# Eighteen products of an output projection moved between the last attention head's steps, and the second norm's product moved to GpSimd and ScalarE

## The chip, the cores and the metric

The kernel runs on one core of a Trainium2 chip. The metric is the device time of one execution in microseconds; the lower the better. A profile names the engines PE (TensorE, its weight loads apart as PEld), DVE (VectorE), ACT (ScalarE), POOL (GpSimd) and SP (SyncE, which here only issues DMAs).

## The reference

A decoder block on 1024 tokens of width 1024, one layer, all in float32:

```python
xn = rmsnorm(h, norm_mix_g);  proj = xn @ w_in
att = forgetting_attention(q, k, v, log_f)        # 8 heads of 64, causal, softmax
sg  = chunked_spatial_gating(u, vg, ...)          # gMLP, chunks of 128
h = h + concat([att, sg]) @ w_out                 # the output projection
h = h + conv_ffn(rmsnorm(h, norm_ffn_g), ...)     # D_FF = 2816
return rmsnorm(h, norm_final_g)
```

The change lies at the end of the attention, in the output projection and in the norm in front of the ConvFFN.

## The kernel before, in words

**Precision.** Every large product is done in three passes: each operand is split into a rounded high part and a low part, and high x high, high x low and low x high are summed in PSUM. So one product of a 128x128 block with 512 columns is three matmul instructions.

**The heads.** Eight heads run one behind the other, five steps each (`STEPS`, 40 in all, `n` from 0 to 39, head `h = n // 5`). A step turns up to two groups of softmax rows for the next step (`turn_p`: four transposes into a PSUM bank, L1026, a high part by ScalarE, L1027, a low part by VectorE, L1028, both into a `pt` buffer, of which there are three), and multiplies the groups of this step by V (`values`, L1042). While a head is worked on, the logits of the next one are made in the steps' gaps (`logits_mm`, L978 and L979; `logits_min` on VectorE, L991; `logits_exp` on ScalarE, L1001). The last head's steps, 35 to 39, have no next head: nothing stands between their turns and products. All PE instructions here are chained by hand in program order (`seq`). PSUM has eight banks: two `place()` tiles of two banks each for logits (tag `L`), and four `bank()` tiles (tag `b`).

**The row tail.** Behind step 37's products, the last head's reciprocal row sums are transposed (L940), copied (L941), stored to HBM (L942) and loaded back as a broadcast (L943). `pair_half(3, ...)` then multiplies the pair of heads 6 and 7 by them and splits the result: L956 on VectorE, L957 on ScalarE, L958 on VectorE, second token half first. The result, `attT[3]`, is the fourth of the four operands of the attention's part of the output projection.

**The output projection.** `wmm(tt, hf, ps, ks_)` (L1279 to L1281) multiplies the token tile `tt` (eight of 128 tokens) with the column half `hf` (512 columns) of the weights `wo[k]`; `k` = 0 to 3 are the four pairs of heads, three products each. The gating's part was done earlier and lies in HBM as `hpd`. `wo_load` (L1087) loads weights and has POOL split them (L1098, L1099). All eight banks are taken (`psb` is released, `psc` opened) and the tiles 0, 4, 1, 5 (`first`) run their k = 0, 1, 2 ahead into them: 72 products. Then, in the order 0, 4, 1, 5, 2, 3, 6, 7, each tile gets its last products, VectorE adds `hpd` per half (`hadd`, L1289), and `norm2` makes the second norm: ScalarE squares with a row sum (L1296) and takes the root (L1297), VectorE inverts it (L1298) and multiplies the tile by it and by the gain in one operation (L1299). `flip` of the tile before turns the normed tile with eight transposes (L1317) and spreads it by ScalarE and VectorE (L1303 to L1334) into operands of a Strassen-like product of the ConvFFN.

**Ahead for the ConvFFN.** `upw_a` and `upw_b` load the first two blocks of up weights; `split` makes high and low parts of A11 and A12 (ScalarE L160, VectorE L166, four of each, called before and after the 72 products); with `inplace`, POOL makes their eight sums (L1251 to L1253 and L1259). The ConvFFN's first products are L1372.

**Order.** Each engine works its queue in order. What the program writes is a list; a scheduler of the framework orders each engine's queue by program order and by its own estimate of what is ready. `after(tc, later, earlier)` forces an order within it. A tile of a pool can be used again when everything that reads or writes it is done.

Of the kernel before, what the change touches and what calls it, by code (L numbers as in the profile page):

```python
# [69 lines left out]
def block_kernel(ctx: ExitStack, tc: tile.TileContext, xT, xtok, wuv, wv0, wva, wvk, wvl, wqk, cpk, bfv,  # L70
# [1030 lines left out]

    STEPS = [[(h, g) for g in GROUPS[n:n + 2]] for h in range(8) for n in range(0, 9, 2)]
# [35 lines left out]
    for n, step in enumerate(STEPS):  # L1138
# [63 lines left out]
    psa.release()  # L1202
    psa = tc.alloc_tile_pool(name="psc", bufs=4, space=bass.MemoryType.PSUM, reuse_waits="tile")
# [39 lines left out]
    def upw_b(i, out, inplace=False):  # L1243
# [5 lines left out]
        if inplace:  # L1249
            s = [a21, ut_(upl, "sg", [P, 512], F32, 4), a11, a12]  # L1250
            pool.tensor_tensor(out=a11, in0=a21, in1=a11, op=ALU.add)  # L1251
            pool.tensor_tensor(out=s[1], in0=a11, in1=a22, op=ALU.add)
            pool.tensor_tensor(out=a21, in0=a21, in1=a22, op=ALU.add)  # L1253
# [5 lines left out]
        pool.tensor_tensor(out=s[3], in0=s[1], in1=a12, op=ALU.add)  # L1259
# [13 lines left out]
    normed = {}  # L1273

    def wmm(tt, hf, ps, ks_):
        ts_ = slice(tt * P, (tt + 1) * P)
        for k in ks_:
            w = wo[k][hf]
            pe.matmul(ps, attT[k][:, 0, ts_], w[:, 0, :], start=(k == 0), stop=False)  # L1279
            pe.matmul(ps, attT[k][:, 0, ts_], w[:, 1, :], start=False, stop=False)  # L1280
            pe.matmul(ps, attT[k][:, 1, ts_], w[:, 0, :], start=False, stop=(k == 3))  # L1281
# [5 lines left out]
    def hadd(tt, hf, ps):  # L1287
        o = slice(hf * 512, hf * 512 + 512)
        x = dve.tensor_tensor(out=h2[tt][:, o], in0=ps, in1=h2[tt][:, o], op=ALU.add)  # L1289
        if tt == 5:  # L1290
            after(tc, x, normed[1])

    def norm2(tt):
        xn[tt] = ut_(xtp, "xn", [P, 1024], F32, 2)
        r = ss2[:, tt:tt + 1]
        act.activation(xn[tt], h2[tt], AF.Square, accum_out=r)  # L1296
        act.activation(r, r, AF.Sqrt, bias=eps[:, 0:1], scale=1.0 / 1024)  # L1297
        dve.reciprocal(r, r)  # L1298
        normed[tt] = dve.scalar_tensor_tensor(out=xn[tt], in0=h2[tt], scalar=r, in1=g2b, op0=ALU.mult, op1=ALU.mult)  # L1299
# [9 lines left out]
    def flip(tt):  # L1309
# [3 lines left out]
        for kh in range(2):  # L1313
            ps = sbank()
            for j in range(4):
                k = 4 * kh + j
                pe.transpose(ps[:, j * P:(j + 1) * P], xn[tt][:, k * P:(k + 1) * P], ident)  # L1317
# [18 lines left out]

    WA = [upw_a(i) for i in range(AHEAD)]
# [481 lines left out]
```

## Time and profile before

| | |
|---|---|
| median of 3 runs | 1049.43 us (1049.25 to 1049.82) |
| the profiled execution | 1049.38 us |
| its span, first to last instruction | 1047.7 us |
| granted TensorE clock, mean | 0.999 |

How to read the profile: its page gives the busy time of every engine as a share of the span; the view by windows gives it for a stretch of time, in us from the span's start; the timeline gives single instructions (start, duration, engine, line, operation, output <- inputs, shape, count when several are merged, and in brackets the idle time before and what ended it). `SPq` and `ACTq` are the queues that issue DMAs. A matmul's shown duration overlaps the next one's, so its price is the distance between starts.

### The profile page before, as it was taken

The page shows a single profiled execution, that of the slowest core. Times are in us where ns is not written, and L with a number is a line of the kernel's source. Part 1 is how long each engine was busy: PE and PEld are TensorE (multiplying, and loading weights), DVE is VectorE, ACT ScalarE, POOL GpSimd, SP SyncE. Part 2 cuts the span into 40 slices and gives each one's busy share as a digit, 9 for nine tenths or more (in the row PEclk, how much of TensorE's full clock was granted, in tenths as well). Part 3 has the DMA queues.
Part 4 walks back from the last instruction along what each step waited for, and adds up shares of the span by engine and source line. Part 5 has one row for each costly group of instructions (what it writes and reads, how often), then busy time and mean ns, then how long its engine had stood idle before and what let it go on. Part 6 is the DMA issues. An engine that isn't in the chain of part 4 may idle for free.

```text
span 1047.7 us, 14269 instructions
## 1 busy us (share of the span) xinstructions
PE 1037.6 (99%) x4998; PEld 869.5 (83%) x4998; DVE 891.8 (85%) x1302; ACT 563.4 (54%) x1003; POOL 217.7 (21%) x165
## 2 busy tenths in 40 slices
PE   9999999999999999999999999999999999999997
PEld 6988888988888888788888888888888888888886
DVE  6898887888888779998999989898997866897774
ACT  6777632457767747644444444444444544454654
POOL 0000241500422540253333323323331000000000
PEclk9999999999999999999999999999999999999999
DMA  9622558795745533232254431432322998333432
GB/s 326 237 87 86 159 155 245 224 260 174 205 138 171 184 139 141 80 103 79 96 174 162 131 121 60 131 121 70 131 81 81 320 336 297 105 98 101 142 119 101
DMA packets 67451, 161.66 MB, mean 154 GB/s; under 512 B 8094, under 2 KB 9238, under 8 KB 67380
## 3 DMA queue, kind: packets, MB, share of 16 engines
q1 hardware_dynamic: 67108, 160.72, 47.7%
q8 instruction: 39, 0.64, 0.3%
q14 instruction: 32, 0.26, 0.1%
q10 hardware_dynamic: 272, 0.04, 0.0%
HBM read 115.68 MB, written 45.05 MB: 153 GB/s over the span
## 4 chain that ended last, share of the span: by engine, by line
PE 92%; DVE 3%; DMA 2%; ACT 1%; issue 1%; SPq 1%; ACTq 0%; DVEq 0%
PE k L1632 20%; PE qc L1372 11%; PE qa L1372 11%; PE qd L1372 11%; PE qb L1372 5%; PE ps L270 5%; PE pb L270 5%; PE pb L1042 3%; PE pb L1026 2%; PE qc L510 2%; PE qa L510 2%; PE qd L510 2%; PE pl L979 2%; PE pl L978 2%; PE pf L1066 1%; PE pf L1068 1%
## 5 line engine op out<-in xcount | busy, mean ns | idle before, releaser
L1632 PE MATMUL k<-whb,wha 128*128 128x512 f32 (+1 forms) x936 | 209.9, 386 | 0.0
L1632 PEld LDWEIGHTS k<-whb,wha 128*128 128x128 f32 x936 | 174.1, 188 | 35.8 <-DVE wha L166 0.2
L1372 PE MATMUL qc<-xT,whb 128*128 128x512 f32 x540 | 129.9, 389 | 0.1
L1372 PE MATMUL qa<-xB,wha 128*128 128x512 f32 x528 | 127.4, 390 | 0.0
L1372 PEld LDWEIGHTS qc<-xT,whb 128*128 128x128 f32 x540 | 101.3, 188 | 21.6 <-ACT whb L160 0.5
L1372 PEld LDWEIGHTS qa<-xB,wha 128*128 128x128 f32 x528 | 98.8, 188 | 20.8 <-DVE wha L166 0.4
L160 ACT CAST wha<-sg 128x512 fp32r<-128x512 f32 x77 | 47.8, 622 | 96.9 <-PE k L1632 83.9
L160 ACT CAST whb<-sg 128x512 fp32r<-128x512 f32 x82 | 50.6, 618 | 87.3 <-PE qc L1372 67.1
L166 DVE TENSOR_TENSOR wha<-sg,wha 128x512 fp32r<-128x512 f32 x77 | 52.8, 687 | 39.2 <-ACT wha L160 39.1
L1372 PE MATMUL qd<-xB,whb 128*128 128x512 f32 x264 | 63.7, 389 | 0.0
L1372 PE MATMUL qd<-xT,whb 128*128 128x512 f32 x264 | 63.7, 389 | 0.0
L1372 PE MATMUL qb<-xT,whb 128*128 128x512 f32 x252 | 61.0, 389 | 0.0
L166 DVE TENSOR_TENSOR whb<-sg,whb 128x512 fp32r<-128x512 f32 x82 | 57.0, 697 | 4.4 <-ACT whb L160 4.3
L1027 ACT CAST pt<-pb 128x512 fp32r<-128x512 f32 x72 | 40.4, 584 | 37.5 <-PE pb L1026 32.5
L1256 POOL TENSOR_TENSOR sg<-raw 128x512 f32<-128x512 f32 x20 | 30.8, 1541 | 140.3 <-DVE whb L166 78.1
L1372 PEld LDWEIGHTS qd<-xT,whb 128*128 128x128 f32 x264 | 49.5, 188 | 10.5 <-DVE u L1479 0.3
L1372 PEld LDWEIGHTS qd<-xB,whb 128*128 128x128 f32 x264 | 49.6, 188 | 10.3
L1028 DVE TENSOR_TENSOR pt<-pb,pt 128x512 fp32r<-128x512 f32 x72 | 47.4, 687 | 10.7 <-ACT pt L1027 10.4
L1372 PEld LDWEIGHTS qb<-xT,whb 128*128 128x128 f32 x252 | 47.2, 188 | 10.0 <-DVE whb L166 0.3
L1042 PE MATMUL pb<-pt,V 128*128 128x512 f32 (+3 forms) x192 | 49.6, 362 | 0.4 <-DVE pt L1028 0.3
L1259 POOL TENSOR_TENSOR sg<-sg,raw 128x512 f32<-128x512 f32 x20 | 33.3, 1667 | 63.5 <-DVE whb L166 63.5
L1257 POOL TENSOR_TENSOR sg<-sg,raw 128x512 f32<-128x512 f32 x20 | 34.8, 1740 | 47.5 <-issue 44.9
(426 smaller groups left out, 2241.1 us busy)
## 6 DMA issues: line engine op xcount, KB each, us to landing
raw<-wup SPq DMA_DIRECT2D x44, 512.0 KB
sg<-hx SPq DMA_DIRECT2D x77, 256.0 KB
hx<-hs SPq DMA_DIRECT2D x44, 256.0 KB
hx<-ca SPq DMA_DIRECT2D x35, 256.0 KB
xT<-wdn SPq DMA_DIRECT2D x28, 256.0 KB
x<-kd SPq DMA_DIRECT2D x24, 256.0 KB
A<-xtok SPq DMA_DIRECT2D x8, 512.0 KB
raw<-wqk SPq DMA_DIRECT2D x8, 512.0 KB
```

The lines of the kernel that those rows point to most:

```text
L160: act.copy(h, src)
L166: return eng.tensor_tensor(out=l, in0=src, in1=f32(h), op=ALU.subtract)
L270: pe.matmul(banks[m], xs(n, xi, k)[:, ms], w[:, wi, :], start=(first and k == 0 and c == 0 and (own or m % 2 == 0)), stop=(k == 3 and c == ...
L510: pe.matmul(ps, w[:, wi, ks], xs(n, xi, k), start=(first and c == 0), stop=(c == 11), skip_group_check=True)
L1027: casts.append(act.copy(pt[:, 0, :], ptr))
L1028: los.append(dve.tensor_tensor(out=pt[:, 1, :], in0=ptr, in1=f32(pt[:, 0, :]), op=ALU.subtract))
L1042: seq(pe.matmul(po[half][:, o:o + w], lhs, pt[:, s, c:c + w], start=(new and s == 0), stop=(s == 1 and (half, k) in ((1, 6), (0, 3))), ski ...
L1256: pool.tensor_tensor(out=s[0], in0=a21, in1=a22, op=ALU.add)
L1257: pool.tensor_tensor(out=s[1], in0=s[0], in1=a11, op=ALU.add)
L1259: pool.tensor_tensor(out=s[3], in0=s[1], in1=a12, op=ALU.add)
L1372: pe.matmul(ps, w[:, wi, ks], xb[:, xi, k, :], start=(first and n == 0), stop=(n == 11), skip_group_check=True)
L1632: pe.matmul((banks[bk + m] if ps is None else ps)[:, o], xh[:, xi, ms], wh[:, wi, o], start=((first and p_ == 0 or new) and n == 0), stop= ...
```

## The change

1. **Early products.** `wmm` moves ahead of the steps and takes an `order` function. A table `EARLY` puts products of token tile 0 behind three steps, chained like the rest: behind step 34, k = 0 and 1 of both halves (12 products), behind step 36, k = 2 of half 0 (3), behind step 37, k = 2 of half 1 (3). They accumulate in `place()` tiles: the logits' last ones are read in step 33 and 34.
2. **Weights.** `wo_load((0, 1))` is called at step 33 and `wo_load((2, 3))` at step 34 behind `pair_half(2, ...)`; both were called at step 35.
3. **PSUM.** `psb` stays until the end of the projection. Each token tile has one 1024-column place (`half_of`), of which there are two; `first` has two tiles (0 and 4) in place of four, so 36 products can run without `attT[3]`. The square writes its (unused) output into the tile's place instead of `xn`. `flip` takes `bank()` tiles and is ordered behind given products; tile 0's flip stands behind the first half of tile 1.
4. **The norm's product.** `hadd` has POOL multiply each half by the gain (`gained`) behind VectorE's sum; `norm2` has ScalarE scale the whole by the inverse root (`Copy` with `scale`). VectorE's L1299 goes.
5. **The weight sums on POOL.** The eight in-place sums are held in `parts` and issued two at a time behind the gain products of tiles 1, 5, 2 and 3.

```diff
+    EARLY = {34: ((0, 0, (0, 1)), (0, 1, (0, 1))), 36: ((0, 0, (2,)),), 37: ((0, 1, (2,)),)}
+    def half_of(tt, hf):
+        if tt not in wide:
+            wide[tt] = place()
+        return wide[tt][:, hf * 512:hf * 512 + 512]
...
-        if h == 7 and s == 0:
+        if n == 33:
             for _ in filler:
                 pass
             wo_load((0, 1))
-            wo_load((2, 3))
...
+        if n == 34:
+            wo_load((2, 3))
...
         fill((h, s))
+        for tt, hf, ks_ in EARLY.get(n, ()):
+            wmm(tt, hf, half_of(tt, hf), ks_, lambda m: seq(m) or m)
+            done.update((tt, hf, k) for k in ks_)
...
-    psa.release()
-    psa = tc.alloc_tile_pool(name="psc", bufs=4, space=bass.MemoryType.PSUM, reuse_waits="tile")
...
-            pool.tensor_tensor(out=a11, in0=a21, in1=a11, op=ALU.add)
-            pool.tensor_tensor(out=s[1], in0=a11, in1=a22, op=ALU.add)
-            pool.tensor_tensor(out=a21, in0=a21, in1=a22, op=ALU.add)
+            sums_ = ((a11, a21, a11), (s[1], a11, a22), (a21, a21, a22), (a12, s[1], a12))
+            ops = [lambda o=o: pool.tensor_tensor(out=o[0], in0=o[1], in1=o[2], op=ALU.add) for o in sums_]
+            parts.extend((ops[:2], ops[2:]))
...
     def hadd(tt, hf, ps):
         o = slice(hf * 512, hf * 512 + 512)
-        x = dve.tensor_tensor(out=h2[tt][:, o], in0=ps, in1=h2[tt][:, o], op=ALU.add)
-        if tt == 5:
-            after(tc, x, normed[1])
+        dve.tensor_tensor(out=h2[tt][:, o], in0=ps, in1=h2[tt][:, o], op=ALU.add)
+        if hf == 0:
+            xn[tt] = ut_(xtp, "xn", [P, 1024], F32, 2)
+        gained[tt] = pool.tensor_tensor(out=xn[tt][:, o], in0=h2[tt][:, o], in1=g2b[:, o], op=ALU.mult)
...
-        act.activation(xn[tt], h2[tt], AF.Square, accum_out=r)
+        act.activation(wide[tt], h2[tt], AF.Square, accum_out=r)
         act.activation(r, r, AF.Sqrt, bias=eps[:, 0:1], scale=1.0 / 1024)
         dve.reciprocal(r, r)
-        normed[tt] = dve.scalar_tensor_tensor(out=xn[tt], in0=h2[tt], scalar=r, in1=g2b, op0=ALU.mult, op1=ALU.mult)
+        act.activation(xn[tt], xn[tt], AF.Copy, scale=r)
...
-    first = (0, 4, 1, 5)
-    banks8 = {(tt, hf): (bank() if hf == 0 else sbank()) for tt in first for hf in range(2)}
+    first = (0, 4)
     for hf in range(2):
         for tt in first:
-            wmm(tt, hf, banks8[tt, hf], (0, 1, 2))
+            wmm(tt, hf, half_of(tt, hf), [k for k in range(3) if (tt, hf, k) not in done])
...
         for hf in range(2):
-            if tt in first:
-                wmm(tt, hf, banks8[tt, hf], (3,))
-                hadd(tt, hf, banks8[tt, hf])
-            else:
-                ps = bank()
-                wmm(tt, hf, ps, range(4))
-                hadd(tt, hf, ps)
+            m = wmm(tt, hf, half_of(tt, hf), (3,) if tt in first else range(4))
+            hadd(tt, hf, half_of(tt, hf))
+            if tt == 1 and hf == 0:
+                flip(0, m)
         norm2(tt)
-        if prev is not None:
-            flip(prev)
+        if prev:
+            flip(prev, m)
         prev = tt
+        if tt in (1, 5, 2, 3):
+            for o in parts.pop(0):
+                after(tc, o(), gained[tt])
...
+    psa.release()
+    psa = tc.alloc_tile_pool(name="psc", bufs=4, space=bass.MemoryType.PSUM, reuse_waits="tile")
```

More of the change, by code (lines that the diff above doesn't have):

```diff
@@ L1100, in wo_load, with wmm @@
             wo.append(w)
+    def wmm(tt, hf, ps, ks_, order=lambda m: m):
+        ts_, m = slice(tt * P, (tt + 1) * P), None
+        for k in ks_:
+            w = wo[k][hf]
+            order(pe.matmul(ps, attT[k][:, 0, ts_], w[:, 0, :], start=(k == 0), stop=False))
+            order(pe.matmul(ps, attT[k][:, 0, ts_], w[:, 1, :], start=False, stop=False))
+            m = order(pe.matmul(ps, attT[k][:, 1, ts_], w[:, 0, :], start=False, stop=(k == 3)))
+        return m
+    def half_of(tt, hf):
[3 more added lines that the diff above has]
+    EARLY = {34: ((0, 0, (0, 1)), (0, 1, (0, 1))), 36: ((0, 0, (2,)),), 37: ((0, 1, (2,)),)}
+    wide, done, gained = {}, set(), {}
     STEPS = [[(h, g) for g in GROUPS[n:n + 2]] for h in range(8) for n in range(0, 9, 2)]
@@ L1258, in upw_b @@
             pool.tensor_tensor(out=s[2], in0=a21, in1=a11, op=ALU.add)
-        pool.tensor_tensor(out=s[3], in0=s[1], in1=a12, op=ALU.add)
+            pool.tensor_tensor(out=s[3], in0=s[1], in1=a12, op=ALU.add)
         src = {"A22": a22, "S1": s[0], "S2": s[1], "S3": s[2], "S4": s[3]}
@@ L1272, in block_kernel @@
     xn = [None] * 8
[L1273 to L1281, printed above, removed]
     def hload(tt):
@@ L1307, in hl_of, with flip @@
         lo_of(n, c, src)
-    def flip(tt):
+    def flip(tt, floor=None):
         c = slice((tt % 4) * P, (tt % 4) * P + P)
@@ L1313, in flip @@
         for kh in range(2):
-            ps = sbank()
+            ps = bank() if floor is not None else sbank()
             for j in range(4):
                 k = 4 * kh + j
-                pe.transpose(ps[:, j * P:(j + 1) * P], xn[tt][:, k * P:(k + 1) * P], ident)
+                t = pe.transpose(ps[:, j * P:(j + 1) * P], xn[tt][:, k * P:(k + 1) * P], ident)
+                if floor is not None:
+                    after(tc, t, floor)
             pp.append(ps.rearrange("p (k t) -> p k t", k=4))
```

2 lines of the change are left out of this document (1 added, 1 removed).

## Prediction

> **What bounds the kernel now.** I read the page first, then the busy time by stage, then TensorE's timeline around the last head, then what it waited for there.
>
> ```profile
> span 1047.7 us, 14269 instructions
> PE 1037.6 (99%) x4998; PEld 869.5 (83%) x4998; DVE 891.8 (85%) x1302; ACT 563.4 (54%) x1003; POOL 217.7 (21%) x165
> ```
> ```profile
> 351.00:361.00 10.00, 8.77 (x56) 6.96 (x55) 7.67 (x14) 7.36 (x17) 4.57 (x5) 1.00 0.48 149
> 361.00:371.00 10.00, 10.00 (x45) 8.25 (x45) 6.66 (x10) 5.38 (x9) 2.61 (x2) 1.00 0.63 231
> 383.00:410.00 27.00, 26.99 (x143) 22.25 (x142) 25.42 (x42) 18.01 (x37) 0.00 (x0) 1.00 0.56 195
> 410.00:431.00 21.00, 21.00 (x102) 17.37 (x102) 20.00 (x28) 15.14 (x24) 0.00 (x0) 1.00 0.07 26
> 431.00:451.00 20.00, 19.87 (x86) 15.70 (x85) 19.19 (x24) 12.30 (x17) 9.10 (x5) 1.00 0.40 130
> ```
> The columns after the window are its length, then busy time (and instructions) of PE, PEld, DVE, ACT, POOL, then the granted clock (1.00 everywhere here). PE is the bound, and the only stretch with a visible hole is 351 to 361, the last head's steps. Behind it the output projection (from 360.8) runs without a hole. The profiled execution took 1049.38 us, the median is 1049.43, so the sum is made on 1049.38.
>
> Two rows of the chain of work give PE's pace: a 512-column product costs 5.47/24 = 0.228 us, a transpose 0.87/8 = 0.109.
>
> ```profile
> 416.87 0.87 PE ps L1317 x8
> 417.74 5.47 PE qa L1372 x24
> ```
> ```profile
> 350.36 0.77 PE L1042 MATMUL pb<-pt,V 128*128 128x384 f32 x4
> 350.96 0.62 PE L1026 MATMUL pb<-ident,H 128*128 128x128 f32 x4
> 352.48 0.66 PE L1026 MATMUL pb<-ident,H 128*128 128x128 f32 x4 [0.89 <-DVE pt L1028]
> ...
> 358.05 0.27 PE L940 MATMUL pb<-ident,rs 128*8 128x128 f32 x1
> ...
> 360.37 0.61 PE L1042 MATMUL pb<-pt,V 128*128 128x384 f32 x3 [0.28 <-DVE pt L1028]
> 360.82 0.45 PE L1279 MATMUL pb<-whl,A 128*128 128x512 f32 x1
> ```
> ```profile
> PEld pb L1026 <- DVE pt L1028: 1.4, 2, 1.1
> ...
> PEld pb L1042 <- DVE pt L1028: 0.7, 2, 0.5
> PEld pb L1042 <- ACT pt L1027: 0.4, 1, 0.4
> ```
> From 350.96 to 360.82 PE does 29 transposes (steps 36 to 39 and the row tail's) and value products worth 18 of 512 columns: 29 x 0.109 + 18 x 0.228 = 7.3 us in 9.9. The wait rows (in total, times, longest) show where. So **about 2.5 us is all that can be filled**: some 1.3 around 352 (four transposes are through at 351.40, the next start at 352.48), 0.3 ahead of 356.6, and 0.7 to 0.9 in step 39.
>
> **The change, part by part.**
>
> *Eighteen products move into the head.* They are 18 x 0.228 = 4.1 us of PE, taken out of the stage from 360.82. Their place must be free and their operands there:
>
> ```profile
> 350.41 0.53 DVE L991 CUSTOM_DVE_ANT_0 gg<-pl,t,lim 128x256 f32<-128x256 f32 x1
> ```
> ```profile
> 344.77 0.33 SPq L1090 DMA_DIRECT2D raw<-woa  x1
> 345.80 2.56 POOL L1099 TENSOR_TENSOR whl<-raw,whl 128x512 fp32r<-128x512 f32 x2
> 349.42 2.54 POOL L1099 TENSOR_TENSOR G<-raw,G 128x512 fp32r<-128x512 f32 x2
> 353.00 2.57 POOL L1099 TENSOR_TENSOR G<-raw,G 128x512 fp32r<-128x512 f32 x2
> ```
> The logits place of j=1 is read until 350.94, as step 34's last value product goes out; weights 0 and 1 are split by 348.4, weight 2 by 352.0, and loading them a step or two sooner in the program keeps that. SP issues the last of these loads at 344.77, and an earlier issue only lets its queue go on sooner; the work on POOL is the same.
>
> Twelve products behind step 34 take 2.74 us and push everything behind them. The chain they meet is PE's own order:
>
> ```profile
> 353.84 0.59 ACT L1027 CAST pt<-pb 128x512 fp32r<-128x512 f32 x1 [0.43 <-PE pb L1042]
> ```
> That cast waits for a `pt` buffer (three of them), that is for a value product two groups back, so ScalarE and VectorE cannot run ahead while PE does the twelve. The pause of 1.3 around 352 is covered, the rest (1.4) is delay. The three products of step 36 add 0.68 and the pause of 0.3 goes: at the row tail, behind 15 early products (3.4 us), PE is 3.4 - 1.5 = **1.9 late**. The three of step 37 add 0.68; step 39 still waits for the cast and low part of transposes that are late too, and I give back 0.1. The head ends 2.5 late, at 363.3: of 4.1 us, 1.6 are hidden.
>
> *The wait for the last head's rows.* From the row tail to the projection's fourth product:
>
> ```profile
> 358.64 0.27 ACTq L942 DMA_DIRECT2D rsd<-t  x1
> 360.82 0.45 SPq L943 DMA_DIRECT2D H<-rsd  x1
> 364.96 1.29 DVE L956 TENSOR_TENSOR H<-H 128x512 f32<-128x512 f32 x2 [2.64 <-DMA H<-rsd]
> 365.69 1.22 ACT L957 CAST G<-H 128x512 fp32r<-128x512 f32 x2 [2.56 <-DVE H L956]
> 366.34 1.29 DVE L958 TENSOR_TENSOR G<-H,G 128x512 fp32r<-128x512 f32 x2
> 366.81 2.18 ACT L160 CAST wha<-raw 128x512 fp32r<-128x512 f32 x4
> 367.55 4.68 DVE L166 TENSOR_TENSOR wha<-raw,wha 128x512 fp32r<-128x512 f32 x4
> ```
> Tile 0 uses the second half of these: high part at 366.91, low part at 367.63. Before, 72 products (16.4 us) lie ahead of the first one that needs them, so nobody waits. After, only two 1024-column places exist, so 36 products can run without the fourth weight, and 18 of those are spent: PE arrives at 363.3 + 4.1 = 367.4. The rows come 1.9 late: 368.8 and 369.55. PE waits 1.4, does two products, waits 0.25 more: **+1.65**. Bounds: 0.7 if tile 4 (first half) goes first; 2.5 if the row transfer, now issued closer to the load of the first `h2` tile, lands up to 0.8 later.
>
> *The wait for a place.* Tile 1 cannot start before tile 0's place is given back, and that is now after two sums and the square, which writes into the place. In the trace this chain is:
>
> ```profile
> 378.11 0.69 DVE L1289 TENSOR_TENSOR pt<-pb,pt 128x512 f32<-128x512 f32 x1 [5.87 <-PE pb L1281]
> 378.79 0.69 DVE L1289 TENSOR_TENSOR pt<-ps,pt 128x512 f32<-128x512 f32 x1
> ```
> ```profile
> 379.51 1.06 ACT L1296 ACTIVATE xn<-pt 128x1024 f32<-128x1024 f32 x1 [10.52 <-DVE pt L1289]
> ```
> First sum to end of square: 2.46 us. Tile 0's last product is out at 370.5, tile 4's six follow until 371.85. But on VectorE the four low parts of the up weights (L166) stand right behind L958 in the order of before; there they had 6 us of room, now the sums queue behind them: 369.55 + 4 x 0.6 = 372.0, and tile 1 starts at 372.0 + 2.46 = 374.5. **+2.6**. If the sums go ahead of them, only hadd 0.69 and square 1.06 stand behind 370.5, and 0.5 is left. I take 2.6: the order of before is the nearest row. From tile 1 on each place has 24 products (5.5 us) to be emptied in, so no more of this.
>
> *The norm's product.* Off VectorE go eight of 1.28; onto POOL come sixteen of 1.29 (the L1251 family's unhindered duration), onto ScalarE eight of about 1.06:
>
> ```profile
> L1299 DVE SCALAR_TENSOR_TENSOR xn<-pt,ss,g2b 128x1024 f32<-128x1024 f32 x8 | 10.2, 1280 | 0.1
> L1296 ACT ACTIVATE xn<-pt 128x1024 f32<-128x1024 f32 x8 | 8.5, 1064 | 14.1 <-DVE pt L1289 14.1
> ```
> The longer route (sum 0.69, product 1.29, scaling 1.06, some 1.5 of queue) is hidden by a tile's 5.5 us of products, except perhaps at tile 0, whose flip comes 2.74 us after tile 1 starts. VectorE was 25.42 of 27 us busy from 383 to 410 and never held PE for long, so PE gains nothing there directly. It can gain what little PE loses up to 451: 86 products and 19.87 us in the last window, some 0.4. Moving POOL's eight sums costs nothing if they are done by 415. I take -0.4 for all this; bounds -1.0 (every such gap goes) and +1.0 (the collisions below).
>
> **Sum:** -4.1 + 2.5 + 1.65 + 2.6 - 0.4 = +2.25: 1049.38 + 2.25 = **1051.6 us**.
>
> A collision speaks against the move. While POOL added two SBUF tiles, VectorE's L166 with two SBUF inputs went slow, four in 4.68 us where the neighbour L958 takes 1.29 for two, and POOL's own took 1.67 for 1.29; the sum L1289 of 378.79, with one input from PSUM, kept 0.69 beside POOL:
>
> ```profile
> 368.32 1.67 POOL L1251 TENSOR_TENSOR raw<-raw,raw 128x512 f32<-128x512 f32 x1 [12.75 <-DVE wha L166]
> ...
> 378.45 1.29 POOL L1259 TENSOR_TENSOR raw<-sg,raw 128x512 f32<-128x512 f32 x1
> ```
> Each such meeting cost VectorE (4.68 - 2.6)/2 = 1.0 us. In tiles 4 to 7 four VectorE operations each have two SBUF inputs; if all 16 met POOL, that is 16 us, more than the 10.2 taken off. [...]
>
> **Rivals.**
> *Sums first* (0.20): the scheduler puts tile 0's sums ahead of the up weights' low parts, or tile 4 first. Then 0.5 stands for 2.6: +0.15, **1049.5**. For it: tile 0's first sum has its product some 2 us before the splits end. Against: the splits come sooner in the program.
> *The pauses are filled and no new wait arises* (0.13): the one that ends not slower. Its place is the arrival of the last head's rows: if the two transfers and the two waits behind them fit into the 18 products left, -4.1 + 2.5 - 0.4 = -2.0, **1047.4**. It decides from the point where the rows are there by 367.4, that is 1.4 us sooner than I work out. Against: 358.05 to 366.91 is 8.9 us, PE's work between is 7.4.
> *VectorE and POOL block each other* (0.14): a flip waits for a late product and PE with it, at +1.4 beyond my -0.4 end: 2.25 + 1.4 = +3.65, **1053.0**. For it: the rows above. Against: PE has 5.5 us per tile to spare.
> *The change does not do what it says* (0.03): the early products wait for weights and the head is only longer, some +4: 1053.4. Against: the weights' rows.
>
> **How the numbers follow.** The forecast has 0.50. About 0.2% (2.1 us, 1051.5) is what a measurement of this kernel can tell from no change, and the forecast lies next to that edge: of its 0.50 I put 0.34 slower and 0.16 same. Sums first: all same. Pauses filled: 0.06 faster, 0.07 same. The last two: 0.17 slower. Faster 0.06, same 0.43, slower 0.51. The range leaves out most of the full gain and the worst blocking: 1048.4 to 1053.6. The forecast's own range is 1050.6 to 1052.6.
>
> **What would show it.** In the profile after: eighteen L1279 to L1281 products before the last value product, the hole at 352 gone, the first product behind the head near 363.3 (right if 363.0 to 363.7); PE idle 1 to 2 us just before the fourth weight's first product, released by ScalarE's L957; PE idle again 1.5 to 3 us before tile 1, released by the square; VectorE's sums of tile 0 behind all four L166. I am wrong if tile 1 starts before 373, or if PE has holes at the flips, or if the rows are there before PE.

## The result, and the profile after

| | before | after |
|---|---|---|
| median | 1049.44 us (1049.25 to 1049.82, 4 runs) | 1062.05 us (1059.79 to 1063.38, 4 runs) |
| the profiled execution | 1049.38 us | 1059.79 us |
| its span | 1047.7 us | 1058.1 us |
| granted TensorE clock, mean | 0.999 | 0.997; in the three other runs 0.995 |

After/before is 1.0118 (95%: 1.0105 to 1.013): the kernel became slower by some 12.6 us, where +2.25 was forecast. The page of after opens with

```profile
span 1058.1 us, 14299 instructions
PE 1040.5 (98%) x4998; PEld 870.9 (82%) x4998; DVE 886.1 (84%) x1294; ACT 571.5 (54%) x1011; POOL 237.1 (22%) x181
```

PE has the same 4998 matmuls, so what was added must be idle time or slower products. Both can be read off. First the view of waits for PE from 360 to 480 (total us, times, longest). Before, it has one row:

```profile
PE pb L1042 <- DVE pt L1028: 0.3, 1, 0.3
```

After, in the same window:

```profile
PE pl L1106 <- DVE pt L1299: 3.9, 3, 2.0
PE qc L1386 <- DVE u L1497: 2.0, 1, 2.0
PE pl L1106 <- ACT pl L1306: 1.6, 3, 0.8
PE pl L1106 <- ACT G L957: 1.4, 1, 1.4
PE qa L1386 <- ACT pl L1306: 1.1, 1, 1.1
```

They add up to 10.0 us. Then the clock: of the stretches behind the head, by windows (columns as in the prediction), one stands out:

```profile
351.00:361.00 10.00, 10.00 (x64) 8.78 (x63) 5.93 (x10) 5.71 (x14) 3.55 (x4) 1.00 0.42 132
361.00:371.00 10.00, 7.95 (x34) 5.28 (x32) 6.48 (x11) 6.11 (x11) 0.00 (x0) 1.00 0.68 238
374.60:378.20 3.60, 3.50 (x9) 2.71 (x10) 0.35 (x3) 2.89 (x7) 3.40 (x3) 0.54 0.78 271
383.00:410.00 27.00, 26.25 (x130) 21.04 (x129) 18.85 (x28) 17.12 (x31) 21.05 (x16) 1.00 0.40 137
410.00:431.00 21.00, 18.61 (x93) 15.13 (x92) 13.14 (x22) 16.05 (x28) 4.65 (x4) 1.00 0.13 51
```

The hole of 351 to 361 is gone (8.77 busy before, 10.00 now). The next ten microseconds, full before, now have 2 us of holes. And from 374.7 on PE ran slow products: they start 0.427 us apart in place of 0.228, and nine of them take 3.75 us (374.70 to 378.45) in place of 2.05, which is 1.7 us more.

The view counts idle time only. By starts (the distance from the start before, less 0.228) the same waits are 11.5 us. In the head, 2.1 us of pauses were filled: it took 2.50 us longer, but holds 20 products more, the eighteen and two of the next ones that slipped in (361.49 and 361.72 below), and 20 x 0.228 - 2.50 = 2.06. So 11.5 of waits + 1.7 of slow products - 2.1 = 11.1. From step 34's last value products to the end of the span the kernel takes 11.3 us more (349.42 to 1058.1, before 350.36 to 1047.7), so nearly all is found. The two spans differ by only 10.4, because after came to the head 0.94 us sooner: it lacks 1.0 us of waits in its first ten microseconds (L270), where the profiles of both kernels and of the experiments differ by as much. Times in two profiles can be compared only after such a shift.

The rest of the median's distance, 1062.05 - 1059.79 = 2.3 us, goes with the lower clock of the other three runs: 0.002 of 1058 us is 2.1 us, about one more such stretch. Those runs have no trace, and their mean clock also counts the end of the kernel, where PE has no work left and the granted clock is 0.50, so that is inferred.

PE's timeline around the places shows who ended each wait (in brackets):

```profile
361.49 0.40 PE L1106 MATMUL pl<-whl,A 128*128 128x512 f32 x1
361.72 0.39 PE L1107 MATMUL pl<-whl,A 128*128 128x512 f32 x1
361.95 0.59 PE L1042 MATMUL pb<-pt,V 128*128 128x384 f32 x3
362.38 0.45 PE L1108 MATMUL pl<-whl,A 128*128 128x512 f32 x1
...
367.65 0.47 PE L1106 MATMUL pl<-G,G 128*128 128x512 f32 x1 [1.40 <-ACT G L957]
368.74 0.65 PE L1108 MATMUL pl<-G,G 128*128 128x512 f32 x2
369.92 0.50 PE L1106 MATMUL pl<-G,G 128*128 128x512 f32 x1 [0.53 <-DVE pt L1299]
370.49 0.39 PE L1108 MATMUL pl<-G,G 128*128 128x512 f32 x1
372.92 0.50 PE L1106 MATMUL pl<-G,G 128*128 128x512 f32 x1 [2.04 <-DVE pt L1299]
374.70 0.65 PE L1106 MATMUL pl<-whl,A 128*128 128x512 f32 x1 [0.82 <-ACT pl L1306]
375.15 0.63 PE L1107 MATMUL pl<-whl,A 128*128 128x512 f32 x1
375.58 0.63 PE L1108 MATMUL pl<-whl,A 128*128 128x512 f32 x1
```

And VectorE and ScalarE there:

```profile
369.17 0.69 DVE L1299 TENSOR_TENSOR pt<-pl,pt 128x512 f32<-128x512 f32 x1 [0.33 <-PE pl L1108]
369.78 2.49 DVE L166 TENSOR_TENSOR wha<-raw,wha 128x512 fp32r<-128x512 f32 x4
372.18 1.28 DVE L1299 TENSOR_TENSOR pt<-pl,pt 128x512 f32<-128x512 f32 x2
373.50 1.03 ACT L1306 ACTIVATE pl<-pt 128x1024 f32<-128x1024 f32 x1 [3.31 <-DVE pt L1299]
```

Tile 4's first half comes first. The product at 369.92 writes the second half of a place; it started only when the sum of the first half (369.17) had read it. The product at 372.92 does the same in the other place, whose first sum stands behind the four low parts (L166). Then tile 1 waits for the square at 373.50. That one is tile 4's: it starts ahead of the last of the four sums (373.93), and tile 0's square follows at 374.65.

### The profile page after: what moved, and what is told of

Read it like the earlier page. It is cut to its first block, busy times and chain, and to the rows that moved or that the text cites. A ratio compares the mean times of both kernels' runs of the same rounds, so it can differ in the third digit from the quotient of the medians.

```text
span 1058.1 us, 14299 instructions
## 1 busy us (share of the span) xinstructions
PE 1040.5 (98%) x4998; PEld 870.9 (82%) x4998; DVE 886.1 (84%) x1294; ACT 571.5 (54%) x1011; POOL 237.1 (22%) x181
## 4 chain that ended last, share of the span: by engine, by line
PE 93%; DVE 4%; ACT 1%; issue 1%; DMA 0%; DVEq 0%; SPq 0%; ACTq 0%
PE k L1646 20%; PE qc L1386 11%; PE qa L1386 11%; PE qd L1386 10%; PE qb L1386 5%; PE pb L270 5%; PE ps L270 5%; PE pb L1042 3%; PE pb L1026 3%; PE qc L510 2%; PE qd L510 2%; PE qa L510 2%; PE pl L979 2%; PE pl L978 2%; PE ps L854 2%; PE pf L1066 1%
## 5 line engine op out<-in xcount | busy, mean ns | idle before, releaser
L166 DVE TENSOR_TENSOR wha<-sg,wha 128x512 fp32r<-128x512 f32 x77 | 53.0, 690 | 39.2 <-ACT wha L160 39.1
L166 DVE TENSOR_TENSOR whb<-sg,whb 128x512 fp32r<-128x512 f32 x82 | 58.2, 711 | 4.4 <-ACT whb L160 4.3
```

Of the source, the lines that this page charges most:

```text
L166: return eng.tensor_tensor(out=l, in0=src, in1=f32(h), op=ALU.subtract)
```

## The experiments

The theory after the trace: the price lies in the places. A 1024-column place is one buffer, so its second half waits for the sum of its first, and tile 1 for the square (**A**). Rivals: the early products delay the head and gain nothing (**B**); the slow products behind a pause are the larger part (**C**); the norm on GpSimd and ScalarE is too long a route (**D**). Each ratio is to runs of the kernel before on the same chip, whose medians were 1048.77 to 1050.08 us. Gains in us are differences of medians; by the ratios they come out up to 0.9 us smaller or larger.

**1. Both halves' products, then both sums.**

```diff
+        ms = [wmm(tt, hf, half_of(tt, hf), (3,) if tt in first else range(4)) for hf in range(2)]
         for hf in range(2):
-            m = wmm(tt, hf, half_of(tt, hf), (3,) if tt in first else range(4))
             hadd(tt, hf, half_of(tt, hf))
```

> The changed kernel, but both halves' products of a tile go out before its two sums. Theory (the place is one buffer of 1024 columns, so the second half's products wait until the first half's sum has read it): the waits ahead of 369.92 (0.7) and 372.92 (2.2) vanish, and so do the waits of 0.76, 0.33 and 1.46 at later tiles; tile 1 starts near 373.6, since the sums still stand behind four L166. That is 1.1 + 2.5 = 3.6 us: 1058.5 if the low clock behind the pause stays, 1056.5 if it goes. Rival (VectorE's order alone holds TensorE): tile 1 as late as before the edit, 1061 to 1062.

Measured 1057.32 us, ratio 1.0081 (1.0061 to 1.0102): 4.7 us less than after. All waits for a half's sum are gone, in the first tiles and in the later ones; tile 1 now waits 2.95 in one piece for the square. A holds for that part.

**2. The up weights' low parts behind the sums of tiles 0 and 4**, and **3. both edits.**

```diff
+                if i < AHEAD:
+                    after(tc, split_of[n], summed[4])
```

The calls of `split` and of POOL's sums move behind tile 4's norm as well.

> The changed kernel, but the four low parts of the up weights (L166) stand on VectorE behind the first sums of tiles 0 and 4 instead of ahead of them. Rival (VectorE's order): tile 1 starts near 372.5 instead of 374.7, the low clock behind the pause goes with it (1.8), 1058. Theory (the place as one buffer): that too, but the waits of 0.76, 0.33 and 1.46 at later tiles stay, so not below 1057. If neither counts: 1062.

> Both edits at once: both halves' products ahead of the sums, and the sums of tiles 0 and 4 ahead of the four L166. Theory: tile 1 starts near 372.3 (2.4 sooner), the later waits of 2.5 us go, the pause is short enough for the full clock (1.8): 1055.3. What is left above the kernel before is the wait for the last head's rows (1.5), the wait for the place (about 2), the first up products' bank (1.2) and VectorE's queue at 473 (2.2). Rival (clock is not a matter of the pause): 1057.

The order alone: 1062.07 us, 1.0126 (1.011 to 1.0141), no gain: tile 1 starts 1.4 us sooner (373.32), but the halves still wait, and the first transposes come 2.2 us late (380.95), just behind ScalarE's scaling. Both together: 1056.17 us, 1.0067 (1.0052 to 1.0082), 1.2 us below experiment 1 with ranges that overlap. So the queue order is a small term at most.

**4. The same kernel with 19 unread products in the pauses** (they write a bank that nobody reads; the outputs are the same).

```diff
+    def idle(n):
+        for _ in range(n):
+            link(pe.matmul(spare, attT[0][:, 0, 0:P], wo[0][0][:, 0, :], start=True, stop=True))
...
+    for n_, (tt, hf) in zip((6, 0, 2, 8), ((4, 0), (0, 0), (4, 1), (0, 1))):
+        idle(n_)
```

> The changed kernel with 19 products more whose result nobody reads, 6, 2, 8 and 3 of them put into TensorE's four pauses between 366 and 375; it computes the same outputs. Theory (the low clock of 0.54 from 374.6 to 378.2 follows from the long pauses): the nine products after 374.7 take 0.228 instead of 0.427 us each, 1.8 us less, 1060. Rival (the clock falls for another reason, or the pauses are not its cause): 1062 or, if the added products delay others, up to 1063.

1062.59 us, 1.0125 (1.011 to 1.014). Inconclusive: the edit also changed VectorE's order, so a pause of 2.5 ahead of tile 1 stayed and a slow stretch followed it. Asked again on the kernel of experiment 3, **5. with 4 and 9 unread products in its two pauses**:

```diff
+        if tt == 0:
+            spare = bank()
+            dummies(4)
+        if tt == 1:
+            dummies(9)
```

> Both edits (products of both halves first, sums ahead of the L166), and 13 products more whose result nobody reads: 4 in the wait for the rows, 9 in the wait ahead of tile 1. Theory (the low clock follows a long pause): no product at 0.427 us after tile 1 has started, 1.8 us less than without the 13, some 1054.3. Rival (the low clock has another cause): as without them, 1056.2.

The profiled executions answer the question. The windows around tile 1, experiment 3:

```profile
374.00:378.00 4.00, 3.21 (x10) 2.55 (x11) 4.00 (x6) 3.41 (x7) 4.00 (x4) 0.73 0.85 287
378.00:382.00 4.00, 4.00 (x17) 3.17 (x16) 2.19 (x3) 1.15 (x1) 0.97 (x1) 0.84 0.68 238
```

and experiment 5:

```profile
374.00:378.00 4.00, 4.00 (x19) 3.30 (x19) 4.00 (x5) 1.79 (x4) 3.36 (x2) 1.00 0.74 263
378.00:382.00 4.00, 4.00 (x28) 3.54 (x27) 3.07 (x6) 3.25 (x6) 1.57 (x2) 1.00 0.53 176
```

With the pause filled the clock stays at 1.00. So the slow stretch comes from the pause and not from the place in the code. What it gains in time is less clear. The profiled execution is 3.2 us shorter (1054.26 against 1057.49), but 1.8 of that lie ahead of the head, where experiment 3's has a wait of 1.4 us near 221; 1.4 are left, near the 1.7 us of a stretch. And the medians do not differ (1056.01 us, 1.0063, 1.005 to 1.0077). Both kernels keep a pause of 2.3 us near 470, in the ConvFFN; a slow stretch behind it in the executions without a trace would explain that, but is not shown. As for **C**: one stretch is 1.7 us of the 12.6, with the inferred second one some 4, so the slow products are not the larger part.

**6. That kernel with VectorE's order in the ConvFFN as before**, and **7. the change itself with that order.** The wait near 470 stands in a stage that the change does not touch. VectorE's timeline of after shows it:

```profile
468.07 1.78 DVE L166 TENSOR_TENSOR whb<-sg,whb 128x512 fp32r<-128x512 f32 x1
...
470.38 2.08 DVE L1438 SCALAR_TENSOR_TENSOR ca<-h,cp,ca 128x1022 f32<-128x1022 f32 x1
472.39 0.68 DVE L166 TENSOR_TENSOR whb<-sg,whb 128x512 fp32r<-128x512 f32 x1
472.99 1.21 DVE L1536 TENSOR_TENSOR ca<-ca,cg 128x1024 f32<-128x1024 f32 x1
474.12 0.67 DVE L1497 TENSOR_TENSOR u<-u,qc 128x512 f32<-128x512 f32 x1
```

PE waits for the last of these. The three in front of it stand there before, too (460.15, 461.78 and 462.38, ahead of the sum at 463.52). New are low parts (L166) that the scheduler put sooner than before, such as the one at 468.07: up to this sum VectorE has one more of them to do. `after` puts them back:

```diff
+            after(tc, low[2, "S2"], mult)
...
+        if i == 1:
+            after(tc, low[2, "S1"], low[2, "S3"])
+            after(tc, low[2, "A22"], conved[NFF + 1])
+            after(tc, low[2, "S4"], low[2, "A22"])
```

> As e12w_filled (both edits and 13 unread products), and VectorE's order in the first three units of the feed-forward part held to that of the kernel before: there seven low parts of the up weights (L166) stand one place or more later, behind the sums that TensorE waits for. Theory (the wait of 2.3 ahead of the third product group near 467 comes from that order alone): it goes, and as no pause over 1.4 is left, no run has a low-clock stretch: 1051.5 to 1052.5, all runs within 1 us. Rival (VectorE is late there for lack of time, not for its order): the wait moves, 1055 to 1056 with the spread as before.

> The changed kernel as it is, with VectorE's order in the first three feed-forward units held to that of the kernel before. Theory: the wait of 2.2 at 472 goes, 1059.5 to 1060. Rival: it moves, 1062.

1052.03 us, 1.0029 (1.0018 to 1.0039), and 1058.56 us, 1.0087 (1.0072 to 1.0103). The waits of PE from 360 to 480 in the first:

```profile
PE pl L1106 <- ACT G L957: 1.6, 1, 1.6
PE qb L1411 <- DVE whb L166: 1.2, 1, 1.2
```

This kernel is the change with halves, order and ConvFFN mended and the pauses filled. Two waits are left, and the 13 unread products still take 13 x 0.228 = 3.0 us. The order of one stage that nobody edited was worth 3.5 us of the 12.6 in the medians (1062.05 to 1058.56), more than the wait of 2.0; between the profiled executions of experiments 5 and 6 it was 2.1. What the rest is, is not shown.

**8. The change without early products.**

```diff
-    EARLY = {34: ((0, 0, (0, 1)), (0, 1, (0, 1))), 36: ((0, 0, (2,)),), 37: ((0, 1, (2,)),)}
+    EARLY = {}
```

> The changed kernel without early products: all of the projection's products behind the head, in places as in the change, with its norm. Theory: no wait for the rows (36 products are 8.2 us), but the waits for a sum and for the place stay in the first and the later tiles (some 1.5 + 0.9 + 2.5), and so do the up product's bank (1.2) and the queue at 473 (2.2): 8 us above before, 1057. Rival (the early products and what they delay are the loss): within 1 us of before.

1058.58 us, 1.0089 (1.0075 to 1.0103): 9.6 us slower than before without an early product, 3.5 faster than with them. B is about a quarter of the whole.

**9. The norm on VectorE as before, the places kept**, and **10. that without early products.**

```diff
-        act.activation(xn[tt], xn[tt], AF.Copy, scale=r)
+        dve.scalar_tensor_tensor(out=xn[tt], in0=h2[tt], scalar=r, in1=g2b, op0=ALU.mult, op1=ALU.mult)
```

> The early products and the places of the change, but the norm as before: its product on VectorE, the square into its own SBUF buffer, GpSimd's eight sums at once. Theory (places): the second halves still wait for their sums; only the square drops out of the wait ahead of tile 1, 1.1 us less, 1060 to 1061. Rival (the norm's move is most of the loss): 1052 or below.

> The places of the change alone: no early product, and the norm as before on VectorE. Theory (a tile in one place costs, and most where VectorE is full): the second halves wait for sums and the places for sums, 2 to 3 us several times with low-clock stretches behind, 1066 to 1069. Rival (the places are harmless, the early products and the norm's move cost): 1049 to 1052.

1072.17 us, 1.0216 (1.0195 to 1.0238), and 1069.61 us, 1.0201 (1.0185 to 1.0216). The first was expected some eleven lower. With the norm, POOL's eight sums are back at their place of before, and the halves' waits, three of them in after, became five:

```profile
PE pl L1106 <- DVE pt L1299: 11.6, 5, 4.2
```

The longest has this cause, by the timelines of VectorE and POOL:

```profile
370.19 4.62 DVE L166 TENSOR_TENSOR wha<-raw,wha 128x512 fp32r<-128x512 f32 x4
374.73 1.28 DVE L1299 TENSOR_TENSOR pt<-pl,pt 128x512 f32<-128x512 f32 x2
```
```profile
370.95 1.64 POOL L1271 TENSOR_TENSOR raw<-raw,raw 128x512 f32<-128x512 f32 x1 [15.77 <-DVE wha L166]
372.67 1.59 POOL L1271 TENSOR_TENSOR sg<-raw,raw 128x512 f32<-128x512 f32 x1
374.22 1.71 POOL L1271 TENSOR_TENSOR raw<-raw 128x512 f32<-128x512 f32 x1
```

The low parts take 4.62 us beside POOL's sums where after had 2.49 with POOL idle, and tile 0's sums stand behind them. Then the clock falls:

```profile
374.00:378.00 4.00, 2.54 (x6) 2.06 (x7) 2.70 (x4) 0.13 (x1) 4.00 (x4) 0.50 0.30 122
```

So D falls in this arrangement: with places, parts 4 and 5 of the change together (the norm's product moved, POOL's sums held back) save some 10 us, 1072.17 against 1062.05. Which of the two saves how much was not tried alone. The four ratios together:

| places in all | early products | none early |
|---|---|---|
| parts 4 and 5 as in the change | 1.0118 | 1.0089 |
| norm and POOL's sums as before | 1.0216 | 1.0201 |

**11. The early products alone, with single banks.** Tiles 0 and 4 keep the places, 1 and 5 and the later ones get 512-column banks, as before; the norm is before's.

```diff
-    first = (0, 4)
+    first = (0, 4, 1, 5)
+    banks8 = {(tt, hf): (half_of(tt, hf) if tt in (0, 4) else bank()) for tt in first for hf in range(2)}
...
+        both = place() if tt not in (6, 7) else None
```

> The eighteen early products with the norm as before (product on VectorE, square not into a place), and with the places given out otherwise: tiles 0 and 4 in the two places, all others in the four 512-column banks, the transposes of the second norm in the places, both halves' products of tiles 0 and 4 ahead of their sums. Then 54 products stand ahead of the first one that needs the last head's rows (12.3 us for the 8 that the rows need), so no wait for rows, none for a place, no second half that waits for a sum. Theory (the early products are worth the pauses that they fill, and the waits behind them are the loss): 1.6 to 2.0 us below the kernel before, some 1047.2. Rival (the head's delay of 2.5 is passed on by something else, the rows or VectorE): level with before or up to 1 us above.

1053.33 us, 1.0034 (1.0021 to 1.0048): 8.7 us better than after, but slower than before, where 1.6 to 2.0 us below it was expected. No place and no row is waited for any more in the projection; what PE waits for is

```profile
PE qc L1389 <- DVE u L1500: 2.1, 1, 2.1
PE ps L1327 <- ACT xtB L1333: 1.0, 1, 1.0
PE pb L1106 <- DVE pt L1298: 0.8, 1, 0.8
PE pl L1327 <- DVE xn L1308: 0.6, 1, 0.6
PE ps L1327 <- DVE xn L1308: 0.4, 1, 0.4
```

the ConvFFN order again (2.1) and 2.8 us around the transposes: for the norm (L1308, 1.0), for ScalarE to copy earlier transposes out of their bank (1.0), and for a bank that a sum has yet to read (0.8). This kernel with the ConvFFN order held was not run; that wait is about half of its distance to before.

**12. The same with the norm on GpSimd and ScalarE and the ConvFFN order of before.**

```diff
+        act.activation(xn[tt], xn[tt], AF.Copy, scale=r)
...
+            ps = wide[tt][kh] if tt == 7 else wide[tt][:, kh * 512:kh * 512 + 512]
```

> The early products, tiles 0 and 4 in places with both halves' products ahead of the sums, all other tiles in 512-column banks, the norm of the change (product on GpSimd, scaling on ScalarE) with its square written into the place that the same tile's transposes use next, and the feed-forward order of before held. Theory (the early products gain the 2.1 us of pauses if no place, sum or row is waited for; the norm's move frees VectorE and costs nothing): 1.5 to 2.5 us below the kernel before, near 1047. Rival (GpSimd's products and VectorE block each other in the projection): holes at the transposes, level with before or above.

1054.69 us, 1.0052 (1.0039 to 1.0065), expected near 1047. The ConvFFN wait is gone, and in its place the transposes wait for ScalarE's scaling:

```profile
PE pl L1331 <- ACT xn L1313: 5.0, 4, 1.9
```

Here D holds: without the places' waits, the longer route is what PE waits for.

**13 to 15. The transposes half a tile to a tile later**; the same without early products; the same with the norm on VectorE.

```diff
+    FLIPS = {(2, 0): (0,), (2, 1): (4,), (3, 0): (1,), (3, 1): (5,), (6, 0): (2,), (6, 1): (3,), (7, 1): (6,)}
...
+                for t_ in FLIPS.get((tt, hf), ()):
+                    flip(t_, m)
```

> As e8p_banks_and_norm, but each tile's transposes stand on TensorE behind the half tile at whose end the norm is there by the trace: tile 0's behind tile 2's first half, tile 4's behind its second, tile 1's and 5's behind the halves of tile 3, 2's and 3's behind those of tile 6, 6's behind tile 7. Theory (the head's pauses, 2.1 us, are a real gain as soon as nobody waits behind them; what e8p lost is the 5.6 us of waits ahead of the transposes and a low-clock stretch): no hole over 0.5 us between 350 and 430, 1046.5 to 1047.5, ratio 0.998. Rival (the gain is given back anyway, at the last tiles or in the feed-forward part): 1049 or more.

> As e9_transposes_later, without the early products: the eighteen stand behind the head again. Theory: 2.0 us above e9_transposes_later, level with the kernel before, 1048.5 to 1049.5. Rival (the early products gain nothing): equal to e9_transposes_later.

> As e9_transposes_later, with the norm as before: its product on VectorE, the square into its own buffer, GpSimd's eight sums at once. Theory (with tiles in 512-column banks VectorE keeps up, as before): within 1 us of e9_transposes_later. Rival (the move of the norm's product is what makes the places and the early products bearable): holes behind VectorE of some 2 us, 1049 to 1050.

1056.56 us, 1.0078 (1.0064 to 1.0092); 1057.42 us, 1.0078 (1.0063 to 1.0092); 1052.27 us, 1.0029 (1.0019 to 1.0038). The first was expected near 1047, the third within 1 us of it. Later transposes gather the waits at the last ones: 5.2 us for ScalarE's scaling (L1313) with the norm moved, and 3.3 with it on VectorE, there for ScalarE's copy (L1339) out of the place that the transposes write. With and without early products the ratio is the same.

**16, 17. POOL's eight sums first**, transposes later still; and without early products.

```diff
+    for p_ in parts:
+        for o in p_:
+            o()
```

> As e9_transposes_later, but GpSimd's eight sums for the up weights run first (from 369 on, beside the products that need nothing of GpSimd) instead of between the norm's products, and each tile's transposes stand half a tile later, with TensorE's order held so. By the trace of e9_transposes_later a tile then has 2.6 us on GpSimd and 1.2 on ScalarE in 5.5 us of products. Theory (GpSimd's queue of sums and products was what gave the gain back): no pause over 1 us between 350 and 430, so no low-clock stretch, 1046.5 to 1047.5. Rival (the last tiles' norms are late whatever the order, as VectorE and ScalarE are full there too): a pause of 2 to 3 us ahead of the last transposes, 1049 to 1051.

> As e11_sums_first without the early products (the scheduler still slips three of them ahead of the last value products). Theory: 1.5 to 2 us above e11_sums_first. Rival (the early products gain nothing): equal.

1059.11 us, 1.0087 (1.0072 to 1.0102), expected near 1047, and 1057.16 us, 1.0073 (1.006 to 1.0086). The theory that POOL's queue makes the last transposes late falls: with the sums out of the way the wait for L1313 was 8.3 in three pieces.

**18. Tiles 0 and 4 finished as soon as the rows are there**, the norm on VectorE.

```diff
+    for tt in (0, 4, 1):
+        for hf in range(2):
+            wmm(tt, hf, banks8[tt, hf], [k for k in range(3) if (tt, hf, k) not in done], link if tt == 1 else lambda m: m)
```

> As e10_same_norm_on_vector (early products, tiles in banks, norm on VectorE as before), but the fourth weight's products of tiles 0 and 4 go out as soon as the last head's rows are there: behind tile 1's first three weights, ahead of tile 5's, some 4 us sooner. VectorE, which stands idle from 371 to 376 in e10_same_norm_on_vector, can then begin the sums and norms sooner. Theory (VectorE and ScalarE work from the first sum to the last transposes without room, and so they, not TensorE, set when the stage ends; the early products gain only if the first sum comes sooner too): the waits of 1.1 and 3.4 us go, and with them the low-clock stretch, 1046.5 to 1048. Rival (the last tiles' chain sum, square, root, product is late by itself): a wait of 2 us or more ahead of the last transposes stays, 1050 or more.

1051.78 us, 1.0033 (1.002 to 1.0045), expected below before. PE waits

```profile
PE pl L1331 <- DVE xn L1311: 2.2, 1, 2.2
PE pb L1106 <- DVE pt L1301: 1.5, 1, 1.5
```

so the work that starts earlier only waits elsewhere. No kernel of the study beats the one before.

## Why the prediction was wrong

The terms of the sum, and what the profile after shows for each, by starts:

| term | forecast, us | after, us |
|---|---|---|
| the head | -4.1 + 2.5 = -1.6 | -2.1 |
| the wait for the last rows | +1.65 | +1.6 |
| the waits ahead of tile 1 | +2.6 | +3.9 |
| later places, and the first up product | 0 | +3.8 |
| VectorE's order in the ConvFFN | 0 | +2.2 |
| slow products | 0 | +1.7 |
| the norm's product | -0.4 | not separable |

**Right: what the head gives.** The head ends 12.96 us behind 349.42 (to 362.38), where before it took 10.46 (350.36 to 360.82): 2.50 late, as forecast, with the hole at 352 filled and the weights there in time. Two more products than forecast stood in it, so it hid 2.1 us and not 1.6.

**Right in size, with some luck: the wait for the last rows.** 1.65 was forecast with tile 0 first, and 0.7 for tile 4 first. Tile 4 went first, and PE still waited 1.40 by the view and 1.56 by starts, ended by ScalarE's L957. Measured from the head, PE came 0.4 us sooner than forecast and the rows some 0.2 later. The rival *the pauses are filled* needed the rows before PE; they were not there.

**Near in time, wrong in cause: the wait for tile 0's place.** Tile 1 was forecast at 374.5, behind all four L166 and tile 0's square; it started at 374.70, which is 375.6 when the 0.94 us are added by which after came sooner to the head, so 1.1 late. And the 2.6 us were put down as one pause behind 371.85. PE did not get that far: it had products of the second halves left and stood still ahead of them, 0.72 and 2.20 us by starts, and only 0.97 was left for the square, which was tile 4's. The sum of the three is 3.9. The step that failed lies ahead of "tile 4's six follow until 371.85": I took the places to be free half by half.

**The step that failed most: "From tile 1 on each place has 24 products (5.5 us) to be emptied in, so no more of this."** It counts from the end of a tile and forgets that the second half needs the sum of the first, which can begin only behind the first half's last product. In place of nothing, after shows 3.8 us by starts: one more such wait (1.46), two small ones for a square (0.76 at 393.66, 0.33 at 406.88), and at the end the first up product waits for a square (1.26). So the 5.5 us were not always enough for the two sums and the square either. With the idle time in brackets:

```profile
414.86 0.50 PE L1106 MATMUL pl<-whl,A 128*128 128x512 f32 x1 [1.30 <-DVE pt L1299]
419.85 1.43 PE L1386 MATMUL qa<-xB,wha 128*128 128x512 f32 x5 [1.09 <-ACT pl L1306]
```

Experiment 1 shows that the halves' rule is the cause: with the two sums behind both halves' products, and nothing else changed in the program, every one of these half waits goes, and the time falls by 4.7 us. The second half lies in another bank. Whether the chip or the framework asks for the wait is not shown: no run has two separate guards in one place.

**Not foreseen: the clock.** Every term of the sum used 0.228 us for a product. In after, the nine from 374.70 on took 3.75 us in place of 2.05, at 0.427 from start to start (granted clock 0.50 from 374.90 to 378.31), so that the 3.9 us of standing still ahead of tile 1 became 5.6. In the profile of experiment 5, with the pause filled, the clock is 1.00 from 360 to 400.

**Not foreseen: VectorE's order in the ConvFFN.** Another wait of 2.0 us (2.2 by starts), some 100 us downstream. The change left that stage's code as it was, but the scheduler gave it another queue order. Experiments 6 and 7 show it by pinning: the wait goes.

**Half right: the norm's product.** "The longer route ... is hidden by a tile's 5.5 us of products" holds in after, where PE is late anyway: together with POOL's later sums the move even saves some 10 us there, of which 2.1 are the low parts' own (4.62 - 2.49 in experiment 9). VectorE's relief is real (383 to 410: 25.42 us busy before, 18.85 after), but it pays only against the places' waits. With single banks (experiments 11, 12) the route is what PE waits for, though these two differ in the ConvFFN order as well.

**The rivals.** The sums stayed behind the low parts, so *sums first* fell; in experiment 2, where they come first, nothing was gained. *VectorE and POOL block each other* shows in single rows only (L1438 2.08 in place of 1.27, L166 1.78 in place of 0.68, both while POOL worked). They stand ahead of the sum that PE waits for in the ConvFFN; no transpose of after waited. The weights were not waited for.

**Where the 2.1 us of filled pauses went.** In after, into the waits above. But no other arrangement kept them either. In the best (experiments 6, 11, 15, 18: +2.9 to +4.4 us in the median) the pause reappears in the rows' arrival, or around the last tiles' transposes: on the route sum, square, root, norm, or at the copies out of the transposes' place. A reading that fits all of them: in the stage from 383 to 410 before had VectorE busy for 25.42 of 27 us, so projecting sooner only makes PE arrive sooner at work that VectorE or ScalarE has yet to do. That is argued; whether some arrangement keeps the gain stays open. Open too: the size of each term alone, since a removed pause also removes its slow stretch (experiment 5: clock 1.00 in place of 0.73 and 0.84; experiments 1 and 2 gain 4.7 and 0, together 5.9).

## What to carry to other kernels

Before work is moved into another buffer, ask what the buffer's unit is: a two-bank tile that holds two results was given back, and waited for, as one here (0.72 and 2.20 us by starts ahead of the second halves of tiles 4 and 0). Add to a pause of TensorE of some 2 us or more 1.7 us for slow products, as measured in after (3.75 us in place of 2.05), which 12 of the 17 such pauses in the table below had, and look at the granted clock of the stretch behind it before the cause is sought in the products there. Compare times of two profiles from a common point, not from the start of the span. And when an engine's list changes, compare the queue orders of stages that were not edited.

## What the runs showed of the hardware

**Pauses and the clock.** Pauses are given here as idle time in the views (by starts a little more: 2.04 is 2.20 in after), with the start of the instruction that ended them.

| pause, us | behind it |
|---|---|
| after: 2.04, to 372.92 | clock 0.50 from 374.90 to 378.31 |
| experiment 1: 2.95, to 374.42 | clock 0.73 in 374 to 378, 0.84 in 378 to 382 |
| 2: 2.23, to 380.95 | 0.84 in 378 to 382, 0.74 in 382 to 386 |
| 3: 2.11, to 374.79 | 0.73 in 374 to 378, 0.84 in 378 to 382 |
| 4: 2.54, to 377.69 | 0.95 in 374 to 378, 0.62 in 378 to 382 |
| 7: 2.04, to 373.50 | products 0.427 apart from 375.87 to 380.99 |
| 9: 4.18, to 375.46 | 0.50 in 374 to 378, 0.65 in 378 to 382 |
| 9: 1.99, to 393.79 | 0.76 in 393 to 400 |
| 14: 5.26, to 417.38 | eight transposes in 1.97 us, 1.09 behind the pause to 405.41 |
| 15: 3.28, to 412.64 | seven products (from 413.46) in 3.03 us, some 1.8 at 0.228 each |
| 18: 2.21, to 411.69 | 0.83 in 410 to 420 |
| 16: three of 2.1 to 3.1, from 390 to 420 | one stretch: 0.88 in 390 to 400, 0.95 in 400 to 410, 1.00 in 410 to 420 |
| after: 2.04, to 474.85 | none: 1.00 in 470 to 480 |
| 11: 2.1, in 451 to 480 | none: 1.00 in 451 to 480 |
| 14: 2.17, to 405.41 | none: products 0.23 apart from 406.57 on |

So 12 of these 17 pauses had a slow stretch. Shorter ones had none in the timelines of after (1.40, 1.30, 1.09) and of the experiments 1 (1.79), 2 (1.65, 1.27), 6 (1.60), 7 (1.80) and 8 (1.81, 1.27). In after the stretch lasted 3.4 us and began 2.0 us behind the end of its pause; the first one of experiment 9 lasted some 6.8 (3.4 us of clock lost in two windows) and began at least 1.4 us before the end of its pause. The price of a product there was 0.427 us in place of 0.228. In before, and in after but for this stretch, the clock was below 1.00 only at the end of the kernel: 0.50 from 1045.4 in before and from 1054.2 in after, where PE's last product had ended at 1041.9 and 1052.2.

**VectorE beside POOL, with two inputs in SBUF each.** In experiment 4 the products of the norm ran beside the low parts:

```profile
371.11 2.99 POOL L1302 TENSOR_TENSOR xn<-pt,g2b 128x512 f32<-128x512 f32 x2 [16.14 <-ACT wha L160]
371.46 4.39 DVE L166 TENSOR_TENSOR wha<-raw,wha 128x512 fp32r<-128x512 f32 x4
```

Four low parts took 4.39 us here and 2.49 in after, where POOL stood still: 1.9 us lost to two products of POOL, about 1.0 each, the size that the prediction had read from the trace of before. (It reckoned with two products of POOL there; three overlap the low parts, the third, from 371.64, for 0.6 us.)
